# Putting the final norm of four tiles into the next product, and moving the FFN transposes by half a step

## The chip, the cores and the metric

The kernel runs on one core of a Trainium2 chip. The core has a matmul engine (TensorE, PE in the profile; its weight loads are PEld), three engines for elementwise work (VectorE or DVE, ScalarE or ACT, GpSimd or POOL) and SyncE (SP), which here issues the DMAs. Each engine works through its own queue in order; semaphores tie the queues together. The metric is the time of one execution on the device, in microseconds. Before the change it is 1392.18 us, the median of three runs (1390.52 to 1394.31).

## What is computed

One layer of a bidirectional encoder on 1024 tokens of width 1024, in float32: a norm, an input projection, gated linear attention in both directions, a pooling branch, a merge with an output projection, and then the part that matters here:

```python
h2 = rmsnorm(x, norm_ffn[l])
gate, up = jnp.split(h2 @ w_ffn_in[l], 2, axis=-1)      # D_FF = 2816
x = x + (jax.nn.silu(gate) * up) @ w_ffn_out[l]
return rmsnorm(x, norm_final)

def rmsnorm(x, g):
    y = x * rsqrt(mean(x * x, axis=-1) + EPS)
    return y * g
```

The final norm scales each token (a row) by its own factor and each column by a gain. In either order of the two multiplications the result is the same up to rounding.

## The kernel before

**Products.** Every float32 operand is split into a high part that the matmul takes exactly and a low part (`split_to`, L196: ScalarE casts the high part at L197, VectorE or GpSimd subtracts for the low part at L198), and a product takes three matmuls: high by high, high by low, low by high (`products`, L268). `mm3` (L273) issues those three and then calls `pump`. The large products are cut into 2 by 2 blocks and made from seven block products (numbered 1 to 7) in place of eight. Products 1, 6, 7 and 4 add up in one set of four PSUM banks, 2, 5 and 3 in another: after a product of a set its sum so far is taken out by `collect`, and the next product of the set goes on adding in the same banks, so its first matmul waits until `collect` has read the bank.

**What sets the order.** The order in each queue is that of the Python program. Side work is woven in by `pump(dt)` (L158), which each `mm3` of 512 columns calls with 1: `soon(delay, step)` (L151) puts a step into the list `put_off`; `pump` takes `dt` off each delay and runs the first steps of the list that have reached zero, in the order in which they were put in. `begin(gen, delay)` (L186) starts a generator; it is advanced whenever its remaining time has run out, and what it yields is added to that time. A step thus gets its place in every queue by the number of `mm3` before it; when it runs depends on its inputs and on what stands ahead of it in its queue.

**The FFN's transposes.** `features(1)` (L1519) is begun just ahead of the first FFN products (L1759). In eight steps `k` it transposes a column block of four normed tiles on PE (L1530) into a PSUM bank (from the pool `ps_g`, five banks, shared with the products 2 and 5 of the FFN), copies it out with the gain on ScalarE (L1533), and after each odd `k` forms differences of blocks on VectorE (L1545, L1548), casts them on ScalarE (`cast_block`, L1511) and subtracts for the low part (`low_block`, L1515). After the eight steps come casts and differences for the blocks of products 3, 7 and 4. Among these steps run the first FFN products; their sums are taken out in `Gated.run`: a copy on ScalarE (L1667), an add on VectorE (L1669), a silu on ScalarE (L1670). The transposes need the norm of tile 7 (ScalarE, L1598) first.

**The last FFN product.** It runs over `OUT_ORDER` = 1, 2, 6, 5, 3, 7, 4. Each product takes six pieces of its inner dimension (five of two blocks, the last of one), so 42 pieces. A piece is loaded from DRAM (`load_piece`, L1731: weights `wor`, activations `gor`, both from SyncE's queue) four pieces ahead, at the head of the loop over pieces, and split three pieces ahead (`split_piece`, L1745), after the second of the four row groups, or after the fourth in a product's last piece: ScalarE casts both, VectorE subtracts for `wor`, GpSimd for `gor`. One row group of a piece takes two `mm3` (one in a product's last piece).

**The final norm.** In the last piece of product 3, `collect` adds each of four sums to its tile of the residual (L1851) and calls `whole(m)` (L1810): the squares on ScalarE with a running sum (`squares`, L1577), then, put off by 2, the scale (`two_scale`, L1582: an add on VectorE at L1584, a power on GpSimd at L1585), and, put off by 1.5 more, two VectorE operations per tile that multiply half a tile by scale and gain (L1822), and the DMA of the tile to the output from SyncE (L1825). In the last piece of product 7, `collect` adds and calls `second_half` for the other four tiles, whose gain is multiplied in on GpSimd (L1833); product 4 ends the kernel with `first_half`.

Tiles of SBUF come from a pool of 39 slots; the residual tile `x2[t]` and the result tile `res` of a norm hold a slot each until their last reader is done.

Of the kernel before, what the change touches and what calls it, by code (L numbers as in the profile page):

```python
# [14 lines left out]
AF = mybir.ActivationFunctionType  # L15
ALU = mybir.AluOpType
# [35 lines left out]
def kernel(  # L52
# [20 lines left out]
    nc = tc.nc  # L73
# [21 lines left out]
    def slot(dtype=F32, shape=(2, HALF), s="slot"):  # L95
        return slots.tile([P, *shape], dtype, tag="slot", name=name(s))
# [7 lines left out]
    def vec(width, s="v"):  # L104
        return small.tile([P, width], F32, tag="vec", name=name(s), bufs=12)

    def bank(pool, s="ps"):
        return pool.tile([P, HALF], F32, tag=pool.name, name=name(s))
# [42 lines left out]
    def soon(delay, *steps):  # L151
        put_off.extend([delay, step] for step in steps)
# [33 lines left out]
    def begin(gen, delay=0.0):  # L186
        side.append([gen, delay])
# [391 lines left out]
    def feature_jobs(c):  # L579
        def restored(i, j):  # L580
            hi, lo = (as_f32(t[:, :, :]) for t in hT.pair(2 * i + c, j))
            whole = slot(s="hs")[:, :, :]
            return whole, (partial(add, whole, hi, lo), None, None)

        def diff(dst, a, b, p=None):
            return partial(sub, dst, a, b), p and dst, p

        b12, job = restored(0, 1)
        yield job
        b11, job = restored(0, 0)  # L590
        yield job
        yield diff(b11, b12, b11)
        b22, job = restored(1, 1)
        yield job
        yield diff(b12, b22, b12)
        yield diff(b22, b22, b11, 6)
        yield None, b12, 7
        yield None, b11, 5
        b21, job = restored(1, 0)
        yield job  # L600
        yield diff(b21, b21, b22, 4)
# [854 lines left out]
    x2 = [None] * NT  # L1456
# [51 lines left out]
    def cast_block(p, i, src):  # L1508
        hi, lo = slot(F32R, s="gh"), slot(F32R, s="gl")
        split_b.setdefault(p, []).append((hi, lo))  # L1510
        nc.scalar.copy(hi[:, :, :], src)  # L1511

    def low_block(p, i, src, eng=nc.vector):
        hi, lo = split_b[p][i]
        eng.tensor_tensor(lo[:, :, :], src, as_f32(hi[:, :, :]), op=ALU.subtract)  # L1515
        if i == 1:
            split_done.add(p)

    def features(half):  # L1519

        for i in range(2):
            blocks[i, half] = [slot(s="hb") for _ in range(2)]

        def block(i, j, c):
            return blocks[i, j][c][:, :, :]

        for k in range(KT):
            ps = bank(ps_g, "tr")
            for i in range(4):
                nc.tensor.transpose(  # L1530
                    ps[:, i * P : (i + 1) * P], xn[4 * half + i][:, k * P : (k + 1) * P], ident[:, :]
                )
            nc.scalar.activation(  # L1533
                blocks[k // 4, half][k % 4 // 2][:, k % 2, :], ps[:, :], AF.Copy, scale=g_ffn[:, k : k + 1]
            )
            i = k % 4 // 2
            if k % 2 and half == 0:
                p, src = (1, block(0, 0, i)) if k < 4 else (2, block(1, 0, i))
                cast_block(p, i, src)
                low_block(p, i, src, nc.gpsimd)  # L1540
            elif k % 2:

                t = block(0, 0, i)
                if k < 4:
                    sub(t, block(0, 1, i), t)  # L1545
                    cast_block(5, i, t)
                else:
                    sub(t, block(1, 1, i), t)  # L1548
                    cast_block(6, i, t)
            elif half and k in (2, 4):  # L1550
                low_block(5, k // 2 - 1, block(0, 0, k // 2 - 1), (nc.gpsimd, nc.vector)[k // 2 - 1])
            elif half and k == 6:
                low_block(6, 0, block(0, 0, 0))
            yield 2 if half == 0 else 2 if k % 2 else 1.2
        if half == 0:
            return

        low_block(6, 1, block(0, 0, 1))
        for i in range(2):
            cast_block(3, i, block(1, 1, i))  # L1560
            yield 2.5
        for p, b in ((7, block(0, 1, 0)), (7, block(0, 1, 1)), (4, block(1, 0, 0)), (4, block(1, 0, 1))):
            i = len(split_b.get(p, ()))
            if p == 7:
                low_block(3, i, block(1, 1, i))
                sub(b, block(1, 1, i), b)
            else:
                low_block(7, i, block(0, 1, i))
                sub(b, b, block(0, 0, i))
            cast_block(p, i, b)  # L1570
            yield 3.5
        for i in range(2):
            low_block(4, i, block(1, 0, i))

    COLS = slice(0, HALF), slice(HALF, D)

    def squares(t, ms, res, j):  # L1577
        nc.scalar.activation(  # L1578
            res[:, COLS[j]], x2[t][:, COLS[j]], AF.Square, scale=1.0 / 32.0, accum_out=ms[:, j : j + 1]
        )  # L1580

    def two_scale(ms):  # L1582
        rs = vec(1, "n3rs")
        nc.vector.tensor_scalar(rs[:, :], ms[:, 0:1], ms[:, 1:2], EPS, op0=ALU.add, op1=ALU.add)  # L1584
        nc.gpsimd.tensor_tensor(rs[:, :], rs[:, :], half_neg[:, :1], op=ALU.pow)  # L1585
        return rs
# [30 lines left out]
    def before_out(p):  # L1617
        if p == 4:
            load_residual(0)
        elif p == 2:  # L1620
            normed()
            begin(features(0), 11.5)
        elif p == 5:
            for _ in range(2):
                units[2].load()
        elif p == 3:
            for _ in range(2):
                units_ahead.step()
# [116 lines left out]
    def split_piece():  # L1745
# [10 lines left out]
            both.append((hi, lo))  # L1756
        ready_pieces.append(both)

    begin(features(1), 12.7)  # L1759
    zs = {n: Gated(units[n], True) for n in range(3)}  # L1760
    out_sums, summing = [OutSums(0)], None

# [34 lines left out]
    x2 = []  # L1797
    gain_final = slot(shape=(D,), s="gfin")
# [9 lines left out]
    scales = {}  # L1808

    def whole(t):  # L1810

        ms, res = vec(4, "n3ms"), slot(shape=(D,), s="res")
        for j in range(2):
            squares(t, ms, res, j)

        def scale():
            rs = two_scale(ms)
            soon(1.5, partial(finish, rs))

        def finish(rs):  # L1820
            for j in range(2):
                nc.vector.scalar_tensor_tensor(  # L1822
                    res[:, COLS[j]], x2[t][:, COLS[j]], rs[:, :], gain_final[:, COLS[j]], op0=ALU.mult, op1=ALU.mult
                )
            nc.sync.dma_start(out[t * P : (t + 1) * P, :], res[:, :])  # L1825

        soon(2, scale)

    def second_half(t):

# [16 lines left out]
    def collect(p, m, ps):  # L1847

        half, j = {1: (0, 0), 2: (0, 0), 6: (0, 1), 5: (1, 1), 7: (1, 1), 3: (0, 1), 4: (1, 0)}[p]
        xs = x2[4 * half + m][:, COLS[j]]  # L1850
        add(xs, ps, xs)  # L1851
        if p == 3:
            whole(m)
        elif p == 7:
            second_half(4 + m)
        elif p == 4:
            first_half(4 + m)
# [71 lines left out]
```

## Time and profile before

| | before |
|---|---|
| median of 3 runs | 1392.18 us (1390.52 to 1394.31) |
| the profiled execution | 1393.17 us |
| its span, first to last instruction | 1391.4 us |
| mean granted TensorE clock | 0.998 |
| HBM traffic over the span | 174 GB/s |
| instructions | 18166 |

The profile is of one execution. Times in its rows are microseconds from the start of the span. A row of the timeline gives start, length, engine, line of the kernel, operation, the tile written and those read, the shape, and in brackets how long the engine idled before and what ended that. `ol` and `oh` are the low and high parts of a piece, `wor` and `gor` its raw loads, `hb` a transposed block, `gh` and `gl` its high and low parts, `n3rs` a token's scale, `x` a residual tile. A row marked SPq is a DMA as SyncE issues it, not its transfer.

### The profile page before, as it was taken

The page shows a single profiled execution, that of the slowest core. Times are in us where ns is not written, and L with a number is a line of the kernel's source. Part 1 is how long each engine was busy: PE and PEld are TensorE (multiplying, and loading weights), DVE is VectorE, ACT ScalarE, POOL GpSimd, SP SyncE. Part 2 cuts the span into 40 slices and gives each one's busy share as a digit, 9 for nine tenths or more (in the row PEclk, how much of TensorE's full clock was granted, in tenths as well). Part 3 has the DMA queues.
Part 4 walks back from the last instruction along what each step waited for, and adds up shares of the span by engine and source line. Part 5 has one row for each costly group of instructions (what it writes and reads, how often), then busy time and mean ns, then how long its engine had stood idle before and what let it go on. Part 6 is the DMA issues. An engine that isn't in the chain of part 4 may idle for free. (4 is left out here: it accounts for less than half of the span.)

```text
span 1391.4 us, 18166 instructions
## 1 busy us (share of the span) xinstructions
PE 1367.6 (98%) x6485; PEld 1143.5 (82%) x6485; DVE 837.3 (60%) x1018; ACT 645.5 (46%) x1176; POOL 750.1 (54%) x556
## 2 busy tenths in 40 slices
PE   8999999999999999999999999999999999999998
PEld 6788999988888888788887788888888888888876
DVE  6364656557736876678783865556556555344464
ACT  6465766655334445554347533333333334443243
POOL 3222717232298546568655276666666667564354
PEclk9999999999999999999999999999999999999999
DMA  6111413312488667996416355555544447965461
GB/s 224 31 53 54 147 60 128 107 47 75 136 242 281 200 209 255 373 403 222 165 57 242 114 174 174 174 175 174 162 151 138 146 142 271 395 246 187 166 238 64
DMA packets 166587, 243.60 MB, mean 175 GB/s; under 512 B 10937, under 2 KB 95969, under 8 KB 166497
## 3 DMA queue, kind: packets, MB, share of 16 engines
q1 hardware_dynamic: 166352, 242.18, 51.3%
q8 instruction: 51, 0.84, 0.2%
q14 instruction: 40, 0.32, 0.1%
q10 hardware_dynamic: 144, 0.26, 0.0%
HBM read 164.55 MB, written 77.86 MB: 174 GB/s over the span
## 5 line engine op out<-in xcount | busy, mean ns | idle before, releaser
L198 POOL TENSOR_TENSOR wl<-fs,wh 128x512 fp32r<-128x512 f32 x120 | 165.8, 1385 | 154.7 <-ACT wh L197 101.8
L271 PE MATMUL ps<-gh,wh 128*128 128x512 f32 x616 | 240.5, 390 | 1.2 <-DVE g L1669 0.6
L271 PE MATMUL ps<-gl,wh 128*128 128x512 f32 x616 | 239.8, 389 | 0.8 <-DVE gl L1515 0.8
L271 PE MATMUL ps<-gh,wl 128*128 128x512 f32 x616 | 239.8, 389 | 0.0
L198 POOL TENSOR_TENSOR wl<-fraw,wh 128x512 fp32r<-128x512 f32 x90 | 129.0, 1433 | 67.5 <-ACT wh L197 59.4
L271 PE MATMUL ps<-hh,wh 128*128 128x512 f32 x376 | 151.7, 403 | 0.0
L271 PE MATMUL ps<-hh,wl 128*128 128x512 f32 x376 | 146.8, 390 | 0.6 <-POOL wl L198 0.6
L271 PE MATMUL ps<-hl,wh 128*128 128x512 f32 x376 | 146.6, 390 | 0.0
L198 POOL TENSOR_TENSOR ol<-gor,oh 128x1024 fp32r<-128x1024 f32 (+1 forms) x42 | 104.5, 2496 | 77.3 <-ACT oh L197 70.3
L271 PEld LDWEIGHTS ps<-gh,wh 128*128 128x128 f32 x616 | 115.7, 188 | 25.9 <-DVE g L1669 0.9
L271 PEld LDWEIGHTS ps<-gl,wh 128*128 128x128 f32 x616 | 115.6, 188 | 24.6 <-DVE gl L1515 1.1
L271 PEld LDWEIGHTS ps<-gh,wl 128*128 128x128 f32 x616 | 115.6, 188 | 24.3 <-DMA wl<-u_out 0.3
L271 PE MATMUL ps<-ol,oh 128*128 128x512 f32 x308 | 120.7, 392 | 2.0 <-DVE ol L198 2.0
L271 PE MATMUL ps<-oh,ol 128*128 128x512 f32 x308 | 120.5, 391 | 0.0
L271 PE MATMUL ps<-oh,oh 128*128 128x512 f32 x308 | 120.4, 391 | 0.0
L198 POOL TENSOR_TENSOR wl<-raw,wh 128x512 fp32r<-128x512 f32 x40 | 54.6, 1377 | 116.2 <-ACT wh L197 107.8
L198 POOL TENSOR_TENSOR wl<-wraw,wh 128x512 fp32r<-128x512 f32 x56 | 89.9, 1632 | 45.6 <-ACT wh L197 45.5
L198 DVE TENSOR_TENSOR ol<-wor,oh 128x1024 fp32r<-128x1024 f32 (+1 forms) x42 | 68.2, 1653 | 47.1 <-ACT oh L197 44.4
L197 ACT CAST wh<-fs 128x512 fp32r<-128x512 f32 x120 | 73.8, 615 | 29.8 <-DVE fs L935 26.3
L271 PEld LDWEIGHTS ps<-hh,wl 128*128 128x128 f32 x376 | 70.6, 188 | 16.2 <-POOL wl L198 1.1
L271 PEld LDWEIGHTS ps<-hh,wh 128*128 128x128 f32 x376 | 70.7, 188 | 13.3 <-ACT wh L197 0.4
L271 PEld LDWEIGHTS ps<-hl,wh 128*128 128x128 f32 x376 | 70.8, 188 | 13.0
(260 smaller groups left out, 3114.5 us busy)
## 6 DMA issues: line engine op xcount, KB each, us to landing
fraw<-in_w_ffn_in_dram SPq DMA_DIRECT2D x44, 512.0 KB, 5.9
gor<-g_out SPq DMA_DIRECT2D x35, 512.0 KB, 5.4
g_out<-s SPq DMA_DIRECT2D x44, 256.0 KB, 2.3
raw<-in_w_in_dram SPq DMA_DIRECT2D x40, 256.0 KB, 4.9
fraw<-in_w_in_dram SPq DMA_DIRECT2D x20, 512.0 KB, 6.6
wor<-t_out SPq DMA_DIRECT2D x20, 512.0 KB
g_out<-g SPq DMA_DIRECT2D x33, 256.0 KB, 2.4
x<-in_x_dram SPq DMA_DIRECT2D x16, 512.0 KB, 4.6
```

The source lines that it names most:

```text
L197: nc.scalar.copy(hi, src)
L198: eng.tensor_tensor(lo, src, as_f32(hi), op=ALU.subtract)
L271: nc.tensor.matmul(ps, a[i], b[j], start=first and n == 0, stop=last and n == 2, skip_group_check=onto)
```

## The change

Two edits. In `features`, the half-1 steps with odd `k` yield 1.6 in place of 2, and the generator is begun with a delay of 13.2 in place of 12.7. In `whole`, the gain is multiplied into the residual tile by one VectorE product of 128x1024, followed by the scale; both are put off by 5 + 5 t for tile t. One ScalarE operation then multiplies the whole tile by its scale into `res`, and the output DMA follows; these are put off by 7.5 + 5 t.

```diff
@@ features
-            yield 2 if half == 0 else 2 if k % 2 else 1.2
+            yield 2 if half == 0 else 1.6 if k % 2 else 1.2
@@
-    begin(features(1), 12.7)
+    begin(features(1), 13.2)
@@ whole
-        def scale():
-            rs = two_scale(ms)
-            soon(1.5, partial(finish, rs))
-
-        def finish(rs):
-            for j in range(2):
-                nc.vector.scalar_tensor_tensor(
-                    res[:, COLS[j]], x2[t][:, COLS[j]], rs[:, :], gain_final[:, COLS[j]], op0=ALU.mult, op1=ALU.mult
-                )
+        def widen():
+            nc.vector.tensor_tensor(x2[t][:, :], x2[t][:, :], gain_final[:, :], op=ALU.mult)
+            scales[t] = two_scale(ms)
+
+        def finish():
+            nc.scalar.activation(res[:, :], x2[t][:, :], AF.Copy, scale=scales[t][:, :])
             nc.sync.dma_start(out[t * P : (t + 1) * P, :], res[:, :])
 
-        soon(2, scale)
+        soon(5 + 5 * t, widen)
+        soon(7.5 + 5 * t, finish)
```

## The prediction

> **What bounds the kernel now.** I read the busy totals first, then the waits of TensorE (PE), then the stages in which it idles.
>
> ```profile
> PE 1367.6 (98%) x6485; PEld 1143.5 (82%) x6485; DVE 837.3 (60%) x1018; ACT 645.5 (46%) x1176; POOL 750.1 (54%) x556
> ```
>
> PE is busy 98% of the span, so the change can only win back time in which PE stood still. Its waits:
>
> ```profile
> PE ps L271 <- DVE ol L198: 2.0, 1, 2.0
> ...
> PE tr L1530 <- ACT xn L1598: 0.9, 1, 0.9
> PE ps L271 <- DVE gl L1515: 0.8, 1, 0.8
> ```
>
> The first lies in the last FFN product, the two others where the transposes of `features(1)` run: the two places of the diff. Next, PE by stage (busy time and records of PE, weight loads, VectorE, ScalarE, GpSimd; then the granted clock), and the matmul before the first stall with the one after:
>
> ```profile
> 800.00:1270.00 470.00, 470.00 (x2075) 389.20 (x2074) 264.88 (x256) 175.49 (x279) 305.92 (x202) 1.00 0.57 193
> ...
> 1336.90:1339.30 2.40, 0.39 (x2) 0.00 (x0) 2.40 (x3) 0.00 (x0) 0.67 (x1) 1.00 0.14 58
> 1339.30:1343.50 4.20, 4.20 (x11) 3.32 (x12) 1.78 (x2) 0.97 (x2) 0.00 (x0) 0.59 1.02 340
> ```
> ```profile
> 1336.90 0.39 PE L271 MATMUL ps<-oh,oh 128*128 128x512 f32 x1
> 1339.30 0.50 PE L271 MATMUL ps<-ol,oh 128*128 128x512 f32 x1 [2.01 <-DVE ol L198]
> ```
>
> 470.00 / 2075 gives 0.2265 us a matmul, 0.68 for the group of three by which `pump` counts (a **unit**). The wait is dearer than its row says: 2.40 - 0.23 = 2.2 us lost, then 11 matmuls in 4.20 us where 2.5 would do, at clock 0.59: 1.7 more. **The first stall costs 3.9 us.** A page bears on this, and nothing below needs it: the Trainium skill (TensorE: Matmul & The Clock Gate, "HAM oscillation — how this bites in real kernels") wants no PE-idle gap beyond about 3.4 us; here 2.40 was enough. By that rule the 1.7 would not be the gap's and would stay, and the sum below would be 1.7 higher.
>
> **The final norm, before.** VectorE, GpSimd, SyncE and ScalarE there (start, length):
>
> ```profile
> 1324.90 1.23 DVE L198 TENSOR_TENSOR ol<-wor,oh 128x1024 fp32r<-128x1024 f32 x1 [2.64 <-issue]
> 1326.05 2.91 DVE L1822 SCALAR_TENSOR_TENSOR res<-x,n3rs,gfin 128x512 f32<-128x512 f32 x1
> 1328.88 0.74 DVE L1822 SCALAR_TENSOR_TENSOR res<-x,n3rs,gfin 128x512 f32<-128x512 f32 x1
> 1331.11 7.00 DVE L1822 SCALAR_TENSOR_TENSOR res<-x,n3rs,gfin 128x512 f32<-128x512 f32 x4
> 1338.04 2.35 DVE L198 TENSOR_TENSOR ol<-wor,oh 128x1024 fp32r<-128x1024 f32 x2
> ...
> 1349.40 2.25 DVE L198 TENSOR_TENSOR ol<-wor,oh 128x1024 fp32r<-128x1024 f32 x1 [1.28 <-ACT oh L197]
> 1352.60 2.73 DVE L1851 TENSOR_TENSOR x<-ps,x 128x512 f32<-128x512 f32 x4 [0.94 <-PE ps L271]
> ```
> ```profile
> 1325.84 2.56 POOL L198 TENSOR_TENSOR ol<-gor,oh 128x1024 fp32r<-128x1024 f32 x1 [3.54 <-ACT oh L197]
> 1329.82 0.99 POOL L1585 TENSOR_TENSOR n3rs<-n3rs,half_neg 128x1 f32<-128x1 f32 x1 [1.42 <-DVE n3rs L1584]
> ...
> 1348.16 2.41 POOL L198 TENSOR_TENSOR ol<-gor,oh 128x1024 fp32r<-128x1024 f32 x1 [3.02 <-ACT oh L197]
> ...
> 1360.13 3.39 POOL L198 TENSOR_TENSOR ol<-gor,oh 128x1024 fp32r<-128x1024 f32 x1
> ```
> ```profile
> 1329.64 8.83 SPq L1825 DMA_DIRECT2D out_dram<-res  x4
> 1338.57 0.38 SPq L1741 DMA_DIRECT2D wor<-t_out  x1
> ...
> 1340.85 0.42 SPq L1741 DMA_DIRECT2D wor<-t_out  x1
> ```
> ```profile
> 1323.78 1.04 ACT L197 CAST oh<-wor 128x1024 fp32r<-128x1024 f32 x1
> ...
> 1342.00 0.62 ACT L197 CAST oh<-wor 128x512 fp32r<-128x512 f32 x1 [12.44 <-DMA wor<-t_out]
> ...
> 1348.31 1.06 ACT L197 CAST oh<-wor 128x1024 fp32r<-128x1024 f32 x1 [0.23 <-DMA wor<-t_out]
> ```
>
> A VectorE operation with two SBUF tensors that meets a GpSimd one waits until that ends: 0.74 alone is 2.91 beside the 2.56 one, and the subtraction at 1349.40 ends at 1351.65, 1.08 after GpSimd at 1350.57. So eight scale-and-gain operations hold VectorE from 1326 to 1338; the subtraction for piece 33 stands behind them, and PE waits for it. And SyncE issues in order: the four output DMAs wait for their tiles until 1338.4, and all later loads behind them.
>
> **What the change does there.** It removes eight operations (12 us of VectorE) and adds four 128x1024 products on VectorE (like `ol`, 1.23 alone) and four ScalarE scalings, priced by the like operation at L1598:
>
> ```profile
> 752.90 1.15 ACT L1598 ACTIVATE xn<-x,n3rs 128x1024 f32<-128x1024 f32 x1 [1.56 <-POOL n3rs L1585]
> ```
>
> Count units from the matmuls whose sum the first `whole` takes (0); tile t's is called at unit t. Piece 33 is first used at unit 28, which PE begins at 1336.9; so it would begin unit 36 at 1342.3, and unit 48, the first of product 4, at 1350.5 if it didn't stall. With their delays the four VectorE products fall due at units 5, 11, 17, 23, the scalings at 8, 14, 20, 26; pieces 33 to 37 are split at 7, 15, 23, 31, 39; loads 35, 36, 37 are issued before units 12, 20, 28. That is the order in each queue, whose work is then done as soon as its inputs are there, often far ahead of PE. With the lengths above, and VectorE and GpSimd taking turns:
>
> - Product 0 waits for GpSimd (1328.4), ends 1329.5. Piece 33's `ol` follows at once: 1330.7, where PE needs it at 1337. **The first stall goes: -3.9.**
> - GpSimd's power 0 waits for that `ol`: 1331.1; scaling 0 ends 1332.3. Product 1 ends 1331.9; GpSimd's part of piece 33 then runs to 1334.2, power 1 to 1334.7, scaling 1 to 1335.8.
> - ScalarE casts piece 34 only now (1335.8 to 1337.8). VectorE's part ends 1338.1, GpSimd's 1340.4 (PE needs it at 1342.8). Product 2 waits for that: 1341.5, product 3 1342.7, power 2 1343.1, scaling 2 1344.3, piece 35's casts 1345.3, scaling 3 **1346.4**.
> - Output DMA 3 waits for scaling 3, and load 37 stands behind it: 1346.85, against 1340.85 now, while PE comes 3.9 earlier. Load 35, behind an output too, took 3.4 us from 1338.57 to its cast; load 37 is 256 KB larger, 0.75 at the 340 GB/s above: I take 4.0, so 1350.8 (ends: 3.4, and the 7.5 that load 37 takes now behind two other pieces).
> - Cast 1351.9, VectorE's `ol` 1353.2. Behind it in VectorE's queue stand the four adds of product 7, whose banks product 4 goes on filling: first add 1353.9, where PE wants to begin at 1350.5. **A second stall of 3.4**, and by the first one's row 1.7 of slow clock.
>
> Sum of this part: -3.9 + 3.4 + 1.7 = **+1.2 us**. From there PE is where it is now or later. GpSimd, whose gain products wait for piece 37, is 2.2 us later than now: piece 38, done at 1363.5 now, comes at 1365.7, and PE, which asks for it in unit 64 at 1365.7 now, asks at 1366.9 after the slow clock; so nothing more is late. Scaling on ScalarE costs nothing itself, since no cast but those named is late by it. The tiles held longer cost nothing: by the code's allocations at most 33 of the 39 slots are in use.
>
> **The transposes.** PE and the chain on VectorE and ScalarE, where `features(1)` runs:
>
> ```profile
> 754.11 0.33 PE L1530 MATMUL tr<-ident,xn 128*128 128x128 f32 x1 [0.87 <-ACT xn L1598]
> ...
> 757.91 0.50 PE L271 MATMUL ps<-gh,wh 128*128 128x512 f32 x1 [0.51 <-DMA wh<-u_out]
> ...
> 766.89 0.50 PE L271 MATMUL ps<-gh,wh 128*128 128x512 f32 x1 [0.62 <-DVE g L1669]
> ...
> 773.58 0.39 PE L271 MATMUL ps<-gh,wl 128*128 128x512 f32 x1
> ...
> 775.31 0.50 PE L271 MATMUL ps<-gl,wh 128*128 128x512 f32 x1 [0.76 <-DVE gl L1515]
> 775.65 0.39 PE L271 MATMUL ps<-gh,wl 128*128 128x512 f32 x1
> ```
> ```profile
> 766.15 0.68 DVE L1669 TENSOR_TENSOR g<-ps,g 128x512 f32<-128x512 f32 x1
> 768.18 1.23 DVE L1548 TENSOR_TENSOR hb<-hb,hb 128x1024 f32<-128x1024 f32 x1 [1.34 <-ACT hb L1533]
> ...
> 774.03 1.23 DVE L1515 TENSOR_TENSOR gl<-hb,gh 128x1024 fp32r<-128x1024 f32 x1 [0.52 <-ACT gh L1511]
> ```
> ```profile
> 764.88 0.68 ACT L1533 ACTIVATE hb<-tr,cols 128x512 f32<-128x512 f32 x1
> 766.87 0.63 ACT L1670 ACTIVATE g<-g 128x512 f32<-128x512 f32 x1 [1.31 <-DVE g L1669]
> 767.41 0.67 ACT L1533 ACTIVATE hb<-tr,cols 128x512 f32<-128x512 f32 x1
> ```
>
> Counted from the start of the FFN, the eight steps stand now after units 13, 14, 16, 18, 20, 21, 23, 24 and the next after 26; then after 14, 15, 16, 18, 19, 20, 22, 23, and 25. The first wait shrinks by one unit, but the weights' DMA at 757.91 stands where it stood and takes that back: 0. The sixth step comes ahead of the add and silu of its unit (766.15, 766.87), so its copy starts at 765.5 and its difference at 766.2, not 768.18. From there by the same lengths: difference 767.4, its cast 768.5, the add 768.0, silu 769.0, the last two copies 769.6 and 770.2, second difference 771.5, its cast 772.55, its `gl` 773.8, which is when PE asks for it; now it ends at 775.26. The three matmuls from 773.58 to 775.65 take 2.07 us where 0.68 would do: **-1.4 us**, with at most 0.1 from the wait at 766.89, whose bank now comes from a copy. Ends: 0 (a cast or bank that I missed holds the chain) and -2.4 (the wait at 766.89, 1.0 with its delays, goes too). What is late next is the steps that follow, moved by a unit: a copy behind a later cast has 0.4 us to spare, the next unit's weights 1.
>
> **Sum.** The profiled execution took 1393.17 us (span 1391.4), 1.0 above the median of 1392.18. 1393.17 + 1.2 - 1.4 = 1393.0; from the median, **1392.0**. About 0.3% (4.2 us) is what a measurement of this kernel can tell from no change: below 1388.0 is faster, above 1396.4 slower.
>
> **Rivals.**
> - *No second stall.* If VectorE and GpSimd meet less often than I lay them out, output 3 leaves earlier; with no waits between the two engines the same sum puts it at 1341.4, and PE then never waits. For it: each meeting hangs on 0.1 to 0.2 us of order. Against: the rows show the wait at every meeting. -3.9 - 1.4: 1386.9. Chance 0.28.
> - *Forecast*: 1392.0, with 1390 if the second gap leaves the clock alone, 1393.5 if the transposes bring nothing (that part then doesn't do what it says). Own range 1389.0 to 1394.5. Chance 0.56.
> - *The second stall outgrows the first.* Load 37 takes 7.5 us as now, since loads 38 and 39 are issued right behind it and share the DMA engines: stall 6.9, so -3.9 + 6.9 + 1.7 - 1.4 = +3.3, 1395.5, and 1396.9 without the transposes' gain. It is slower than before once the load takes over 4.2 us. For it: 7.5 is its row. Against: that load has 35 and 36 ahead, which the change sends off earlier. Chance 0.16, of which 0.10 above 1396.4, where the transposes bring nothing or the clock stays slow for longer after the longer gap.
>
> Faster 0.28 (the first rival), same 0.56 + 0.06 = 0.62, slower 0.10. The range runs from the first rival with the larger gain of the transposes (-3.9 - 2.4) to the lower price of the last: 1386.0 to 1396.0.
>
> **What would show it.** First stall: no PE wait on `ol` L198, the third `ol` after 1318 ending far ahead of PE. Second stall: PE waits on DVE x L1851 at the start of product 4, the load of piece 37 behind the fourth output DMA, a slow clock after it. Transposes: no PE wait on `gl` L1515, that on `xn` about halved, that on the weights' DMA longer. I am wrong if output 3 leaves before about 1343, if loads pass waiting outputs, or if PE waits anywhere else.

## The result, and the profile after

In alternating executions the changed kernel took 1395.32 us (median of 14, 1393.64 to 1397.91), the kernel before 1392.32 us (14, 1390.52 to 1394.5): a ratio of 1.0019, 95% interval 1.0011 to 1.0027. The change makes the kernel about 2.7 us slower (1.5 to 3.8). The profiled execution after took 1396.07 us, 2.9 more than that of before.

The waits of PE after the change (engine, line, what it waited for; total, times, longest):

```profile
PE ps L271 <- DVE x L1849: 5.2, 1, 5.2
...
PE ps L271 <- DMA wh<-u_out: 1.1, 1, 1.1
...
PE tr L1530 <- ACT hb L1533: 0.7, 1, 0.7
...
PE tr L1530 <- ACT xn L1598: 0.2, 1, 0.2
```

The wait on `ol` is gone, and that on `gl` too; in their place stands one of 5.2 on the adds (L1849 now, L1851 before). PE around it, the last matmul ahead of the wait, the first ones behind it and the end of the slow stretch:

```profile
1348.82 0.39 PE L271 MATMUL ps<-oh,ol 128*128 128x512 f32 x1
1354.46 0.77 PE L271 MATMUL ps<-oh,oh 128*128 128x512 f32 x1 [5.25 <-DVE x L1849]
1355.02 0.63 PE L271 MATMUL ps<-ol,oh 128*128 128x512 f32 x1
...
1360.57 0.42 PE L271 MATMUL ps<-oh,ol 128*128 128x512 f32 x1
```

5.64 from start to start, less the 0.23 of one matmul: 5.4 us lost. Then 14 matmuls take 6.11 us (1354.46 to 1360.57) where 3.17 would do: 2.9 more. The granted clock in that place, the seventh column of the windows:

```profile
1353.00:1356.00 3.00, 1.54 (x4) 1.28 (x5) 3.00 (x5) 2.35 (x6) 2.17 (x1) 0.63 1.02 418
1356.00:1360.00 4.00, 4.00 (x11) 3.13 (x10) 2.00 (x3) 4.00 (x8) 4.00 (x4) 0.50 0.91 358
```

What led to it, read from SyncE, ScalarE and VectorE in turn. SyncE's queue (the two last output DMAs, then load 37 with its two transfers, then load 38):

```profile
1342.77 2.42 SPq L1822 DMA_DIRECT2D out_dram<-res  x2
1345.28 0.38 SPq L1741 DMA_DIRECT2D wor<-t_out  x1
1345.77 0.73 SPq L1742 DMA_DIRECT2D gor<-g_out  x1
1346.56 0.45 SPq L1741 DMA_DIRECT2D wor<-t_out  x1
```

ScalarE: scalings 2 and 3 (L1821) with the casts of piece 35 between them and those of piece 36 behind, then the cast of piece 37:

```profile
1341.59 1.15 ACT L1821 ACTIVATE res<-x,n3rs 128x1024 f32<-128x1024 f32 x1 [5.34 <-POOL n3rs L1585]
1342.65 0.60 ACT L197 CAST oh<-wor 128x512 fp32r<-128x512 f32 x1
...
1343.68 1.15 ACT L1821 ACTIVATE res<-x,n3rs 128x1024 f32<-128x1024 f32 x1
1344.73 1.03 ACT L197 CAST oh<-wor 128x1024 fp32r<-128x1024 f32 x1
...
1351.41 1.04 ACT L197 CAST oh<-wor 128x1024 fp32r<-128x1024 f32 x1 [4.69 <-DMA wor<-t_out]
```

VectorE: the subtraction for piece 37, and behind it the four adds for which PE waits:

```profile
1352.48 1.23 DVE L198 TENSOR_TENSOR ol<-wor,oh 128x1024 fp32r<-128x1024 f32 x1 [5.46 <-ACT oh L197]
1353.63 2.48 DVE L1849 TENSOR_TENSOR x<-ps,x 128x512 f32<-128x512 f32 x4
```

Load 37 leaves at 1345.28, as soon as scaling 3 has ended (1344.83) and its output has been issued; its first tile is cast 6.1 us later. The last place is `features(1)`: in the window that held 103 matmul records and 21.15 us of busy PE before (752 to 776) stand now

```profile
752.00:776.00 24.00, 21.96 (x109) 17.15 (x108) 12.54 (x14) 17.31 (x24) 4.23 (x3) 1.00 0.71 252
```

six matmuls more, 6 x 0.2265 = 1.4 us won. It is seen again from the last add ahead of the FFN to the first add of product 3, after:

```profile
749.82 0.68 DVE L1605 TENSOR_TENSOR x<-ps,x 128x512 f32<-128x512 f32 x1
...
1317.29 2.73 DVE L1849 TENSOR_TENSOR x<-ps,x 128x512 f32<-128x512 f32 x4 [14.64 <-PE ps L271]
```

That is 567.47 us, and 568.84 before (749.90 to 1318.74). All traces agree: 568.87 in E2 below, which lacks the transposes' part, and 567.42 to 567.61 in the nine others, which have it.

So the time of the profiled executions adds up: -3.9 (first stall) + 5.4 + 2.9 (second stall and its clock) - 1.4 (transposes) = +3.0, measured +2.9.

### The profile page after: what moved, and what is told of

Read it like the earlier page. It is cut to its first block, busy times and chain, and to the rows that moved or that the text cites. A ratio compares the mean times of both kernels' runs of the same rounds, so it can differ in the third digit from the quotient of the medians.

```text
span 1394.3 us, 18165 instructions
## 1 busy us (share of the span) xinstructions
PE 1368.1 (98%) x6485; PEld 1144.4 (82%) x6485; DVE 831.7 (60%) x1014; ACT 649.4 (47%) x1180; POOL 750.7 (54%) x556
```

## Experiments

Theory: the two parts do separate things; the loss is the second stall, and its chain is scaling 3, output DMA 3, load 37, cast, `ol`, adds. Rivals: the transposes lose, not the norm; or the scalings on ScalarE hold up the casts themselves, whatever the loads do. For each run "lost" below is what PE lost from product 3's adds on, worked out as above from the starts of its matmuls; it is 3.9 before and 8.3 after, and 0 would be PE at its pace. Where product 3's adds begin differs by up to 2 us between profiled executions with the same program ahead of them (1316.92 in E3, 1318.92 in E9), and nearly all of that arises ahead of the FFN, so "lost" tells more than the span.

### E1 and E2: one part at a time

E1 is the kernel before with only the two numbers of `features(1)`; E2 is the changed kernel with those two numbers put back.

```diff
@@ E1: before
-            yield 2 if half == 0 else 2 if k % 2 else 1.2
+            yield 2 if half == 0 else 1.6 if k % 2 else 1.2
-    begin(features(1), 12.7)
+    begin(features(1), 13.2)
@@ E2: after
-            yield 2 if half == 0 else 1.6 if k % 2 else 1.2
+            yield 2 if half == 0 else 2 if k % 2 else 1.2
-    begin(features(1), 13.2)
+    begin(features(1), 12.7)
```

> The kernel before with the transposes' part of the change alone. Theory (two parts that add up; the transposes win 1.4 us, the norm loses 4.4): about 1.4 us below the kernel before, ratio 0.999, no PE wait on gl at L1515, the first stall on ol (2.0 us in the row, 3.9 with the slow clock) unchanged. Rival (the PE time won at the transposes is given back later in the FFN): within 0.3 us of the kernel before.

> The changed kernel without the transposes' part. Theory: first stall gone (-3.9), second stall of about 5.4 us and slow clock of about 3.0 after it, so +4.4 us against the kernel before, ratio 1.003. Rival (the second stall is the size it is because the transposes shift PE against the loads): the stall comes out near the forecast 3.4 and the time near +1.2.

E1: 1392.7 us, ratio 0.9992 (0.9983 to 1.0000) against 1393.78; lost 3.9, as before. E2: 1396.42 us, ratio 1.0024 (1.0015 to 1.0033); lost 6.6 (4.9 and 1.7 of slow clock). The waits of PE that tell them apart, in E1, then in E2:

```profile
PE ps L271 <- DVE ol L198: 2.0, 1, 2.0
PE ps L271 <- DMA wh<-u_out: 1.3, 1, 1.3
```
```profile
PE ps L271 <- DVE x L1849: 4.7, 1, 4.7
```

The transposes alone gain about 1 us (0 to 2.4) and the norm alone loses about 3 (2.1 to 4.6): the first rival falls. In E2 too the wait on `ol` goes and a larger one on the adds comes. It loses less than the 4.4 us expected: in its trace 6.6 - 3.9 = 2.7, since its stall was 4.9 and not 5.4, and its slow clock took 1.7 and not 3.0.

### E3 and E4: the output DMAs out of load 37's way

```diff
@@ E3: after
-            nc.sync.dma_start(out[t * P : (t + 1) * P, :], res[:, :])
+            nc.scalar.dma_start(out[t * P : (t + 1) * P, :], res[:, :])
@@ E4: after
-            nc.sync.dma_start(out[t * P : (t + 1) * P, :], res[:, :])
+            outputs.append((out[t * P : (t + 1) * P, :], res[:, :]))
@@ the last product's loop, behind its load_piece()
+            while n == n_of * 6 and outputs:
+                nc.sync.dma_start(*outputs.pop(0))
```

> The changed kernel with the four output DMAs of the put-off norm issued from ScalarE's queue in place of SyncE's. Theory (loads stand behind outputs in SyncE's queue): load 37 leaves SyncE as soon as its slots are free, 10 us earlier or more, no second stall, -3.9 - 1.4 = -5.3 us against the kernel before, ratio 0.996. Rival 1 (the scalings hold up the casts and splits themselves): the second stall stays, +3. Rival 2 (the outputs' 2 MB hold up the loads on the DMA engines, whatever the queue): a stall of 1 to 3 us is left, time between -3 and +1.

> The changed kernel with the four output DMAs kept in SyncE's queue but issued behind the last load of the product (piece 41). Theory: as with the outputs on ScalarE's queue, no second stall, -5.3 us against the kernel before, ratio 0.996, if four transfers of 0.5 MB still end before the kernel does. Rival 1 (scalings hold up the casts): the stall stays, +3. Rival 2 (traffic): -5.3 here but not with the outputs on ScalarE's queue.

E3: 1394.02 us, ratio 1.0001 (0.9993 to 1.001); lost 4.3. E4: 1391.66 us, ratio 0.9986 (0.9977 to 0.9994); lost 2.6. Both better than the change, E4 better than before, but neither as good as the theory wanted: PE still waits on the adds, 3.5 us in E3 and 1.8 in E4. ScalarE and VectorE in E4, where load 37 leaves at 1332.22:

```profile
1342.79 1.15 ACT L1821 ACTIVATE res<-x,n3rs 128x1024 f32<-128x1024 f32 x1 [5.23 <-POOL n3rs L1585]
...
1344.88 1.15 ACT L1821 ACTIVATE res<-x,n3rs 128x1024 f32<-128x1024 f32 x1
1345.93 1.04 ACT L197 CAST oh<-wor 128x1024 fp32r<-128x1024 f32 x1
...
1347.82 1.05 ACT L197 CAST oh<-wor 128x1024 fp32r<-128x1024 f32 x1
```
```profile
1348.90 2.67 DVE L198 TENSOR_TENSOR ol<-wor,oh 128x1024 fp32r<-128x1024 f32 x1 [0.67 <-ACT oh L197]
1351.50 2.47 DVE L1849 TENSOR_TENSOR x<-ps,x 128x512 f32<-128x512 f32 x4
```

No cast waits for a DMA now. But six casts, those of pieces 35 to 37, stand behind scaling 2, four of them behind scaling 3, and ScalarE stands idle for 5.23 us ahead of scaling 2 until GpSimd's power for it is done. Piece 37 is cast at 1347.82, its subtraction runs beside GpSimd's for piece 36 (2.67 in place of 1.23), and the adds come at 1351.50, 32.9 after product 3's adds (1318.59 there), against 36.3 in the change. The second rival is true as well: the scalings hold piece 37 twice, through SyncE's queue and through ScalarE's.

### E5: load 37 alone on the DMA engines

```diff
@@ load_piece, after
+        if len(loaded_pieces) == 38:
+            hold = slot(shape=(D,), s="hold")
+            nc.sync.dma_start(hold[0:1, 0:HALF], w[0:1, 0, 0:HALF])
+            nc.sync.dma_start(hold[1:2, 0:HALF], g[0:1, 0, 0:HALF])
```

> The changed kernel with a hold in SyncE's queue behind load 37: two copies of one 2 KB row each, from the two tiles that load 37 fills, stand ahead of load 38, so that loads 38 to 41 leave only once load 37 has landed. Theory (load 37 took 6.1 us in place of 4.0 because the loads right behind it share the DMA engines): issue to cast falls from 6.1 to about 4.0, the wait of PE on the adds from 5.2 to about 3.2, and with a slow clock of 1.7 to 3.0 behind it the time is 1392.5 to 1394 (ratio 1.000 to 1.001), unless piece 38 then comes late. Rival (6.1 is what a load of this size takes there, alone or not): 6 us and a wait of 5 stay, ratio 1.002 or above.

1395.61 us, ratio 1.001 (1.0001 to 1.0019) against 1393.89; lost 6.1. Load 37 on SyncE and its cast on ScalarE:

```profile
1346.11 0.38 SPq L1741 DMA_DIRECT2D wor<-t_out  x1
1346.60 0.73 SPq L1742 DMA_DIRECT2D gor<-g_out  x1
```
```profile
1351.22 1.04 ACT L197 CAST oh<-wor 128x1024 fp32r<-128x1024 f32 x1 [3.68 <-DMA wor<-t_out]
```

5.1 us from issue to cast, where it took 6.1 in the change with loads 38 to 40 behind it. Two more runs have that order in SyncE's queue, E2 above and E6 below, and there it took 5.6 (1347.40 to 1353.02) and 5.7 (1346.54 to 1352.20). So sharing with the loads behind is worth 0.5 to 1.0 of the 2.1 us by which the landing was underestimated, and not all of it; neither the 4.0 of the theory nor the 6 of its rival came out. The rest is mostly bytes, which is an estimate and not a test: by the windows of 1 us in E5, the DMA engines moved 0.53 MB from 1344 to 1346, one of the two outputs of 512 KB ahead, and 1.57 MB from 1346 until the cast, the other output and both tiles of load 37, 1 MB. At the 340 GB/s of the prediction that is 4.6 us. The prediction had counted 256 KB beyond load 35's; both tiles together, it is 512 KB. PE loses 4.4 in the gap, and 1.7 more go to the slow clock.

### E6 and E7: the adds ahead of piece 37's subtraction

One VectorE instruction is moved behind the four adds; E7 is the same on top of E4.

```diff
@@ split_piece, after (E6) and E4 (E7)
+            if n == 37 and eng is nc.vector:
+                nc.scalar.copy(hi[:, :c, :], src[:, :c, :])
+                late.append((lo[:, :c, :], src[:, :c, :], hi[:, :c, :].bitcast(F32)))
+            else:
                 split_to(hi[:, :c, :], lo[:, :c, :], src[:, :c, :], eng)
@@ the last product's loop, behind collect(p, m, ...)
+                if m == 3 and n == 35:
+                    lo, src, hi = late.pop()
+                    nc.vector.tensor_tensor(lo, src, hi, op=ALU.subtract)
```

> The changed kernel with one instruction moved: VectorE's low-part subtraction for piece 37 stands behind the four adds of product 7 in its queue, where it stood ahead of them; outputs and loads stay as they are. Theory (PE stands still only because the adds wait behind that subtraction; piece 37 itself is first used 8 units, 5.4 us, later): the wait on the adds goes, PE asks for piece 37 at about 1354.5 in the after trace's time and waits 1.5 us for GpSimd's part, -3.9 - 1.4 + 1.5 = -3.8, ratio 0.997, 0.998 with a slow clock. Rival (the late landing of load 37 sets the time whatever stands behind it): the wait moves to piece 37 at about its old size, over 3 us, ratio 1.000 or above.

> Both edits: the four output DMAs leave behind load 41, and VectorE's subtraction for piece 37 stands behind product 7's adds. Theory (these two queues are all that is left of the second stall): no PE wait over 0.4 us in the last product, -3.9 - 1.4 = -5.3, less 0.3 for a wait on GpSimd: 1387 to 1387.5, ratio 0.996 to 0.9965. Rival (a further wait takes their place, piece 37 or 38 on GpSimd above all): a wait of 1 us or more shows there, ratio 0.9975 or above.

E6: 1396.8 us, ratio 1.0023 (1.0014 to 1.0032); lost 8.3. E7: 1393.48 us, ratio 0.9992 (0.9983 to 1.0000); lost 4.6. Both miss the theory's numbers. The wait on the adds is gone in both, as expected; another has come, on GpSimd. PE and GpSimd in E6:

```profile
1357.05 0.50 PE L271 MATMUL ps<-oh,ol 128*128 128x512 f32 x1 [0.66 <-POOL ol L198]
1367.73 0.79 PE L271 MATMUL ps<-oh,ol 128*128 128x512 f32 x1 [4.94 <-POOL ol L198]
```
```profile
1354.60 2.39 POOL L198 TENSOR_TENSOR ol<-gor,oh 128x1024 fp32r<-128x1024 f32 x1 [4.05 <-ACT oh L197]
1356.95 7.98 POOL L1835 TENSOR_TENSOR x<-x,gfin 128x512 f32<-128x512 f32 x4
1364.89 7.43 POOL L198 TENSOR_TENSOR ol<-gor,oh 128x1024 fp32r<-128x1024 f32 x3
```

GpSimd works without a pause from 1354.60: its part of piece 37, four gain products of the last four tiles (8 us), then its part of piece 38, for which PE waits. A late piece 37 is paid for on PE either at the adds or here; with PE held at the adds, GpSimd had the time to catch up. So the place of one subtraction isn't the cause, and what has to come earlier is piece 37 as a whole.

### E8, E9 and E10: the scalings of tiles 2 and 3 behind piece 37's casts

E8 is E4 with these two scalings put off; E9 is the change with the same and nothing else, so that each output DMA goes with its scaling; E10 puts off the one of tile 3 alone. E9's two due units are those of E8, 40 and 42, since the delays in the diff are the same (its expectation below counts them as 41 and 43).

```diff
@@ whole, E4 (E8) and after (E9)
-        soon(7.5 + 5 * t, finish)
+        if t < 2:
+            soon(7.5 + 5 * t, finish)
+        else:
+            late_scalings.append(finish)
+        if t == 3:
+            soon(37, late_scalings[0])
+            soon(39, late_scalings[1])
@@ whole, after (E10)
-        soon(7.5 + 5 * t, finish)
+        soon(7.5 + 5 * t if t < 3 else 39, finish)
```

> Outputs late as before, VectorE's order as in the change, but the scalings of tiles 2 and 3 stand on ScalarE behind the casts of piece 37 (due at units 40 and 42 in place of 20 and 26). Theory (the 1.8 us that stayed with the outputs out of the way come from ScalarE: the casts of pieces 35 to 37 stand behind scalings that wait for VectorE and GpSimd in turn): the subtraction for piece 37 ends before about 1349.5 in place of 1351.5 and the wait on the adds falls to under 0.5 us, ratio 0.996 to 0.997. Rival (the loads or GpSimd's queue set that time): the wait of 1.8 stays, ratio about 0.9986.

> The change with two due times altered and nothing else: the scalings of tiles 2 and 3, each with its output DMA, fall due at units 41 and 43 in place of 20 and 26, behind the casts of piece 37 on ScalarE and behind load 38 on SyncE. Theory (the place of these two scalings in both queues is the whole of the second stall, and where the outputs stand behind that does not matter): no PE wait on the adds, at most 1 us for GpSimd's part of piece 38, -3.9 - 1.4 = -5.3 or up to 1 less, ratio 0.996 to 0.997. Rival (the outputs must leave behind load 41 as well, since tiles 0 and 1 still hold loads 36 and 37): a wait of over 1.5 us on the adds or on piece 38, ratio 0.998 or above.

> Only the scaling of tile 3 with its output is put off (due at unit 42); that of tile 2 stays at unit 20, ahead of the casts of pieces 35 to 37 and of load 37. Theory: load 37 then waits for output 2, whose scaling ends at about 1343.9 in place of 1344.9, so it leaves 2 us earlier than in the change, lands at 1349.5 to 1350, and PE waits 3 to 4 us on the adds in place of 5.2; with no or one slow-clock stretch of 1.5 behind it, 3.5 to 5 lost in place of before's 3.9: ratio 0.9985 to 1.0005. Rival (output 3 alone is what holds load 37): the wait goes as in the run with both put off, ratio 0.997 or below.

E8: 1388.73 us, ratio 0.9964 (0.995 to 0.9977) against 1393.89; lost 0. E9: 1389.32 us, ratio 0.9973 (0.9963 to 0.9983) against 1393.24; lost 0. E10: 1392.07 us, ratio 0.9993 (0.9984 to 1.0002); lost 2.6, its wait on the adds 2.3. In E9 no wait in the last product is left. SyncE there (load 38, then outputs 2 and 3), ScalarE (the casts of piece 37, then both scalings) and VectorE (piece 37's subtraction, then the adds):

```profile
1338.74 0.64 SPq L1741 DMA_DIRECT2D wor<-t_out  x1
...
1348.17 1.38 SPq L1822 DMA_DIRECT2D out_dram<-res  x2
```
```profile
1344.77 1.05 ACT L197 CAST oh<-wor 128x1024 fp32r<-128x1024 f32 x1 [0.21 <-DMA wor<-t_out]
1346.04 1.05 ACT L197 CAST oh<-gor 128x1024 fp32r<-128x1024 f32 x1 [0.21 <-DMA gor<-g_out]
1346.99 2.19 ACT L1821 ACTIVATE res<-x,n3rs 128x1024 f32<-128x1024 f32 x2
```
```profile
1345.86 3.40 DVE L198 TENSOR_TENSOR ol<-wor,oh 128x1024 fp32r<-128x1024 f32 x1 [1.21 <-ACT oh L197]
1349.18 2.47 DVE L1855 TENSOR_TENSOR x<-ps,x 128x512 f32<-128x512 f32 x4
```

The two scalings with their outputs now come behind load 38 and behind the casts of piece 37, and the adds are done when PE needs them. E9's rival falls: outputs 0 and 1 may stay ahead of the loads. E9 gained 3.9 us on before (2.4 to 5.2), less than its theory wanted; its trace gains 5.3 from the FFN on, as it should, and loses 1.6 ahead of it (the last add ahead of the FFN at 751.48, 749.90 before), where the change does nothing.

In E10 load 37 leaves at 1343.38, behind output 2, and its cast ends a wait of ScalarE for the load:

```profile
1348.64 1.05 ACT L197 CAST oh<-wor 128x1024 fp32r<-128x1024 f32 x1 [2.79 <-DMA wor<-t_out]
```

The wait shrinks from 5.2 to 2.3 and doesn't go. That is less than the 3 to 4 expected, since the load also took less, 5.3 us from issue to cast in place of 6.1; the theory's order holds (both scalings put off: 0; one: 2.3; none: 5.2). E8 and E9 are both faster than the kernel before and than the change; their intervals overlap.

## Why the prediction was wrong

The forecast was 1392.0 (own range 1389.0 to 1394.5, range 1386 to 1396); 1395.3 lies inside the range and 0.2 us below its third rival.

- **First stall.** Right: 3.9 lost before, none after.
- **The order in the queues up to load 37.** Right to 0.15 us. Everything came 1.45 earlier than forecast, nearly all of it because the transposes' gain of 1.4 had been left out of those times; with 1.45 taken off, product 0 was to end at 1328.05 (1328.02), the subtraction behind it at 1329.25 (1329.28), scaling 3 at 1344.95 (1344.83), and load 37 was to leave at 1345.4 (1345.28).
- **Load 37's landing: the step that failed.** "I take 4.0", worked out from the 3.4 of load 35, a load half as large, plus its extra bytes at full rate. It took 6.1, and so the stall was 5.4 in place of 3.4. Load 35 had one output of 512 KB ahead and 512 KB of its own; load 37 had as much ahead and 1 MB of its own, and the forecast added 256 KB. The row of load 37 itself said 7.5, which was kept as an end and as the third rival. The argument against that rival was that loads 35 and 36 leave earlier; but two output DMAs of 512 KB now stand where they stood, and loads 38 to 40 behind. E5, against the change, E2 and E6, puts the loads behind at 0.5 to 1.0. That this rival's time came within 0.2 us is luck: it had a stall of 6.9 and a slow clock of 1.7 where there were 5.4 and 2.9.
- **Slow clock after the second stall.** Taken over as 1.7 from the first stall; it was 2.9. The sum of this part was to be +1.2 and is +4.4, of which 2.0 are the landing and 1.2 the clock. The rival named a longer slow stretch behind a longer gap, and priced only its upper part for it. The length wasn't the reason: E2, with a gap of 5.13, lost 1.7 to the clock. What was is in the last section.
- **"Scaling on ScalarE costs nothing itself."** Wrong, though hidden in the change as it stands: E4 shows that with load 37 sent off 13.6 after product 3's adds in place of 28.0, 2.6 us are still lost, because pieces 35 to 37 are cast behind scalings that wait for GpSimd; E8 shows 0 lost when they aren't.
- **"So nothing more is late" on GpSimd.** It held only because PE stood still at the adds. E6 shows that piece 38 is late once PE doesn't.
- **Transposes.** Right in each step: -1.4 (568.84 to 567.47 us up to product 3's adds; E1 0.9992). The wait on `xn` fell from 0.9 to 0.2 and the weights' DMA took it back, 0.5 to 1.1; the wait of 0.6 on the add at 766.89 became one of 0.7 on the copy that the forecast names.

The direction of the norm's part was right and its size too small, so that a forecast of no change became a loss of 3 us.

## What to carry to other kernels

Where two transfers compare, take the row of the one that has the same neighbours in the queue and not the one that looks cleanest: a load of the same size with transfers on both sides of it took 6.1 us in the change and 7.5 before, the half-size one 3.4. When work moves to an engine because that engine has idle time (ScalarE was busy 46%), look at what stands behind it in the queue while it waits for its own input: here the due times of two 1.15 us scalings decided between 8.3 us lost and none. And a stall that is taken away by reordering one instruction may only move to the next engine in the chain; ask when the data are there, not which instruction waits for them.

## What the runs showed of the hardware

The clock after a gap did not follow the length of the gap. What it did follow can be read from the granted clock in the windows (seventh column). Before, and below it in the change:

```profile
1336.65:1340.06 3.41, 1.40 (x6) 0.85 (x5) 3.41 (x3) 0.00 (x0) 0.92 (x1) 1.00 0.36 132
1340.06:1343.47 3.41, 3.41 (x9) 2.65 (x9) 1.02 (x2) 0.94 (x2) 0.00 (x0) 0.50 0.98 323
1343.47:1346.89 3.42, 3.42 (x16) 2.79 (x16) 0.00 (x0) 1.35 (x2) 1.29 (x1) 1.00 0.97 356
```
```profile
1350.36:1353.77 3.41, 0.00 (x0) 0.00 (x0) 1.29 (x2) 2.09 (x2) 0.00 (x0) 1.00 0.95 384
1353.77:1360.60 6.83, 6.14 (x15) 4.82 (x16) 4.83 (x6) 6.20 (x12) 6.77 (x4) 0.50 0.90 358
1360.60:1364.01 3.41, 3.41 (x17) 2.82 (x16) 3.41 (x2) 3.08 (x5) 3.41 (x3) 1.00 0.03 10
```

The clock is 0.50 for 3.41 us before and for 6.83, twice as long, after the change. It falls once more behind the last matmuls, at 1387.85 before and at 1391.32 in the change: 44.4 and 30.7 us after it had risen, 13 and 9 times 3.413. In every trace here the times between its changes are whole multiples of 3.413 us, so it changes on a fixed grid, and the gaps can be laid over it (gap from start to start of the matmuls; idle, from 0.23 after the last start, in the window of the grid that holds most of the gap):

| run | gap | idle in that window | clock at 0.5 behind it |
|---|---|---|---|
| E10 | 2.69 | 1.84 | none |
| E4 | 2.20 | 1.97 | none |
| E3 | 3.88 | 2.06 | none |
| before, E1 | 2.40 | 2.17 | 3.41 |
| E7 | 3.11 | 2.50 | 3.41 |
| E5 | 4.62 | 2.55 | 3.41 |
| E6 | 5.33 | 2.80 | 6.83 |
| E2 | 5.13 | 3.25 | 3.41 |
| after | 5.64 | 3.41 | 6.83 |

In these ten gaps a window with 2.17 us or more of idle PE was followed by half clock, from its end on, and one with 2.06 or less was not. By this reading E3's 3.88 goes free because the grid cuts it in two, 2.06 and 1.59. Ten gaps of one kernel show no more than that; the limit between 2.06 and 2.17 was not tested by moving a gap on purpose. The slow clock lasted one window where PE was back before it began (0.16 to 1.21 us before), and two where PE came back only after that (0.69 us after in the change, 2.30 in E6). One window cost PE 1.7 to 1.8 us, two cost 2.3 in E6, where PE stood still for part of them, and 2.9 in the change. The Trainium skill (TensorE: Matmul & The Clock Gate, "HAM oscillation — how this bites in real kernels") puts the limit at an idle gap of about 3.4 us; here 2.40 and 3.11 were enough, and 3.88 was not.

So the price of a stall hangs in part on where it falls against the grid, which no line of the program sets. In E3 the profiled execution was the fastest of its eleven runs; nine of them have a lower granted clock (0.996 to 0.998 over the span, 0.999 in the profiled one) and take 1.5 to 4.2 us longer, so most of them probably lost more than the 4.3 of its trace; they were not profiled.

The prediction's turns between VectorE and GpSimd were seen too: the power of 128x1 on GpSimd (0.55 alone) took 1.46 beside the VectorE subtraction that ran from 1328.07 to 1329.28, so that even a tiny GpSimd operation waits its turn:

```profile
1328.23 1.46 POOL L1585 TENSOR_TENSOR n3rs<-n3rs,half_neg 128x1 f32<-128x1 f32 x1 [1.29 <-DVE n3rs L1584]
...
1332.63 0.55 POOL L1585 TENSOR_TENSOR n3rs<-n3rs,half_neg 128x1 f32<-128x1 f32 x1
```
